# A hybrid attention trunk on one core: part of its bulk loads issued on ScalarE's queue and not on SyncE's

## The chip, the core and the metric

The kernel runs on one core of a Trainium2 chip. A core has a matrix engine (TensorE, "PE" in the rows, with its weight loads as "PEld"), a vector engine (VectorE, "DVE"), an activation engine (ScalarE, "ACT"), a general engine (GpSimd, "POOL") and SyncE ("SP"), which computes nothing and here issues the transfers. Each engine works through its own instructions in the order in which they were laid out, and an instruction that waits for a semaphore holds up those behind it. The transfers themselves are carried by 16 DMA engines. "PEq", "SPq" and "ACTq" in the rows are the instruction queues of the engines. The metric is the time of one execution of the whole program in microseconds (us).

## What is computed

One layer on 1024 rows of 1024 numbers, in float32: a root-mean-square norm, one input projection, two groups of mixers side by side, an output projection with a residual add, a dense SwiGLU feed-forward part, and a last norm.

```python
h = rms_norm(x, attn_norm)
a_conv, q, kc_r, vc_r, ks, vs, kw, vw, g = jnp.split(h @ w_in, splits, axis=-1)
conv_out = conv_mixer(a_conv, conv_w, conv_b, conv_ln_g, conv_ln_b)
kc = compress(kc_r, cmp_k_pe, cmp_k_w1, cmp_k_w2)
vc = compress(vc_r, cmp_v_pe, cmp_v_w1, cmp_v_w2)
nsa_out = nsa_attention(q, kc, vc, ks, vs, kw, vw, sigmoid(g))
x = x + concatenate([conv_out, nsa_out]) @ w_out
h = rms_norm(x, ffn_norm)
gate, up = jnp.split(h @ w_gate_up, 2, axis=-1)
return rms_norm(x + (silu(gate) * up) @ w_down, final_norm)
```

The attention has 12 query heads in 4 groups and three gated branches: over compressed blocks, over the 8 best blocks of 64 keys, and over a window of 512 keys, each with a distance penalty.

## The kernel before

A float32 operand of a matmul is split into a rounded part and a rest (`w_hi` and `w_lo`, `ph` and `pl`), and a product is three matmuls. `load_w` (L214) brings weights: it takes one of two `w_raw` buffers, loads 512 KB into it by a transfer that SP issues (L224), lets ACT round it (L225) and POOL subtract, in four pieces (L229). In the first half of the attention POOL first writes one column of the buffer from a result of the attention (L220), so that loads do not run far ahead of it. `Feed` (L193) asks for loads up to two ahead of the one in use.

The stages in order of time: norm, transposes and the first half of the projections; then the attention (`attention`, L678), woven by `weave` (L175) with other matrix work that fills TensorE. The attention has 64 steps: half of the rows (`part`), group, query tile of 128 rows and branch. A step loads its keys and values when they change (L697 to L706) and its queries (`q`, L713 to L720); scores (L756 to L760), minimum (DVE, L764), exponential (ACT, L767), scaling by gate and sum (POOL, L777); then for each block of 128 keys a transpose into PSUM (L783), a split by ACT and DVE (L233) and two products (L800, L801), which stand two blocks behind the transpose (`LAG = 2`, L816). `cmp_stage` (L597) makes the compressed branch and stores it (L644), to be loaded again as `pct` (L727).

The fill is `fill_all` (L1339): first `fill_b` (L938), the second half of the projections, with 18 loads of `w_in` in 22 transfers, stores of the results by SP (L299, L429), then the output projection of the first half of the rows: `mix_in` (L1034) loads the mixed rows, `x_in` (L1020) the residual rows in 8 transfers of 256 KB, `out_loads` 8 loads of `w_out`, `load_row` (L1083) the norm's row, and then feed-forward work (`ffn`). Nearly all of the transfers of the whole program are issued by SP, whatever their size.

The order in which each engine gets its instructions is worked out when the program is built, by a scheduler that plays the program through with modelled times (`schedule_with_timeline_sim=True`) and, when an engine is free, takes what is ready, first that which stands first in the source. So an edit in one place can shift the order elsewhere.

Of the kernel before, what the change touches and what calls it, by code (L numbers as in the profile page):

```python
# [19 lines left out]
P = 128  # L20
# [68 lines left out]
def tile_hymba(ctx: ExitStack, tc, x, attn_norm, w_in, conv_w, conv_b, conv_ln_g, conv_ln_b,  # L89
# [3 lines left out]
    dve, act, pool, pe, sp = nc.vector, nc.scalar, nc.gpsimd, nc.tensor, nc.sync  # L93
# [116 lines left out]
        return bank(name, turn[1][turn[0] % len(turn[1])])  # L210

    pace = []

    def load_w(parts, a, b, eng=pool):  # L214
        raw = wp.tile([P, WCH], F32, tag="raw", name="w_raw", bufs=2)
        hi = wp.tile([P, WCH], F32R, tag="whi", name="w_hi")
        lo = wp.tile([P, WCH], F32R, tag="wlo", name="w_lo")
        back = PACE_B if phase[0] == 0 else PACE_C
        if len(pace) >= back > 0:
            pool.tensor_copy(raw[:, 0:1], pace[-back][:, 0:1])  # L220
        n = a * b
        v = raw[:, :n].rearrange("p (k c) -> p k c", k=a)
        for c, src in parts:
            sp.dma_start(v[:, :, c:c + src.shape[-1]], src.rearrange("(k p) c -> p k c", p=P))  # L224
        act.copy(hi[:, :n], raw[:, :n])  # L225
        step = n // PIECES if eng is pool else n
        for c in range(0, n, step):
            q = slice(c, c + step)
            eng.tensor_sub(lo[:, q], raw[:, q], hi[:, q].bitcast(F32))  # L229
        return (hi[:, :n].rearrange("p (k c) -> p k c", k=a), lo[:, :n].rearrange("p (k c) -> p k c", k=a))  # L230
# [4 lines left out]
    def norm_rows(dst, src, grow, p, tmp):  # L235
        ss = p.tile([P, 1], F32, tag="ss", name="ss", bufs=4)
        act.activation(tmp, src, AF.Square, accum_out=ss)
        rs = p.tile([P, 1], F32, tag="rs", name="rs", bufs=4)
        dve.tensor_scalar(rs, ss, 1.0 / DM, EPS, op0=ALU.mult, op1=ALU.add)
        pool.tensor_tensor(rs, rs, mhalf, op=ALU.pow)  # L240
        dve.scalar_tensor_tensor(dst, src, rs, grow, op0=ALU.mult, op1=ALU.mult)
        return rs

    def transpose_tile(src, hhi, hlo, col, tag="t"):
        for jj in range(2):
            b = bank("tp", tag)
            for k in range(4):
                pe.transpose(b[:, k * P:(k + 1) * P], src[:, (jj * 4 + k) * P:(jj * 4 + k + 1) * P], ident)
            b3 = b.rearrange("p (k t) -> p k t", k=4)
            done = split(hhi[jj][:, :, col:col + P], hlo[jj][:, :, col:col + P], b3)  # L250
        return done
# [24 lines left out]
    def win_chunk(c0):  # L276
        return load_w([(0, w_in[0, :, c0:c0 + P])], KT, P)


    def value_loads(c0, g0, eng=pool):  # L280
        return [lambda kh=kh: load_w([(0, w_in[0, kh * 512:(kh + 1) * 512, c0:c0 + 256]),
                                      (256, w_in[0, kh * 512:(kh + 1) * 512, C_G + g0:C_G + g0 + 18])], 4, 274, eng)
                for kh in range(2)]
# [23 lines left out]
    def values(feed, g0, dst, hf):  # L307
        ws = [feed.get(), feed.get(1)]
        for t in range(hf * 4, hf * 4 + 4):
            yield from value_tile(ws, g0, dst, t)  # L310
        value_gates(g0, hf)
# [103 lines left out]
    def project_d(feed, dst, row, halves, scaled=False):  # L415
        wh, wl = feed.get()
        for hf in halves:
            o = acc_bank("zo")
            yield from gemm_t(o, wh, wl, hf)
            zh = p1.tile([P, 512], F32R, tag="zh", name="zh", bufs=2)  # L420
            zl = p1.tile([P, 512], F32R, tag="zl", name="zl", bufs=2)
            if scaled:
                sc = qsc[:, row // P:row // P + 1]
                act.mul(zh, o, sc)
                dve.scalar_tensor_tensor(zl, o, sc, zh.bitcast(F32), op0=ALU.mult, op1=ALU.subtract)
            else:
                split(zh, zl, o)
            for i, z in ((0, zh), (1, zl)):
                sp.dma_start(dst[i, row:row + P, hf * 512:(hf + 1) * 512], z.bitcast(F32))  # L429
# [86 lines left out]
    def conv_loads():  # L516
        return [lambda c=c: win_chunk(c) for ct in range(2) for c in (CONV + ct * P, ct * P)]

    def conv_in(feed, hf, wide=False):
        y = py.tile([P, 2, 30 + 512], F32, tag="y", name="y")  # L520
        pool.tensor_copy(y[:, :, 0:30], tail)
        for ct in range(2):
            os = []
            for s in range(2):
                os.append(acc_bank("cv"))
                wh, wl = feed.get()
                yield from gemm_t(os[s], wh, wl, hf)
            sg = p1.tile([P, 512], F32, tag="zh", name="sg", bufs=2)
            act.activation(sg, os[0], AF.Sigmoid)
            dve.tensor_mul(y[:, ct, 30:], os[1], sg)  # L530
        if hf == 0:
            pool.tensor_copy(tail, y[:, :, 512:])
        ys[hf] = y
# [326 lines left out]
    def q_load(m):  # L860
        return lambda: win_chunk(C_Q + m * P)

    def kv_loads():
        return [lambda c=c, m=m: win_chunk(c + m * P) for m in range(2) for c in (C_KW, C_KS)]
# [70 lines left out]
    pc_stack, pc = open_pool("pc", "right")  # L935
    turn[1] = "z"

    def fill_b():  # L938
        f1 = Feed([q_load(0), q_load(1)] + value_loads(C_VS, 0) + [q_load(2)] + value_loads(C_VW, 18)
                  + [q_load(m) for m in (3, 4, 5)] + kv_loads() + conv_loads())  # L940
        for m in (0, 1):
            yield from project_d(f1, q_d, m * P, (1,), True)
        yield from values(f1, 0, vs_d, 1)
        done.add(("q", 0))
        yield from project_d(f1, q_d, 2 * P, (1,), True)
        done.add(("q", 1))
        yield from values(f1, 18, vw_d, 1)
        done.update({("v", 0), ("v", 1)})
        for m in (3, 4):
            yield from project_d(f1, q_d, m * P, (1,), True)  # L950
        done.add(("q", 2))
        yield from project_d(f1, q_d, 5 * P, (1,), True)
        done.add(("q", 3))
        for dst in (kw_d, ks_d):
            yield from project_d(f1, dst, 0, (1,))
        done.add(("kv", 0))
        for dst in (kw_d, ks_d):
            yield from project_d(f1, dst, P, (1,))
        done.add(("kv", 1))
        yield from conv_in(f1, 1)  # L960
        done.add(("conv", "in"))
# [53 lines left out]
    def set_in(si, p):  # L1015
        acts[si] = p
        pairs = [p.tile([P, 2, DM], F32, tag="x1", name="x1", bufs=2) for _ in range(2)]
        x1s[si] = [pairs[j // 2][:, j % 2, :] for j in range(4)]

    def x_in(si, ch):  # L1020
        h = slice(ch * 512, (ch + 1) * 512)
        for t, x1 in zip(SETS[si], x1s[si]):
            sp.dma_start(x1[:, h], x[0, t * P:(t + 1) * P, h])

    def set_norm(si, p):
        pools[si] = p
# [3 lines left out]
    def mixed(si, kq):  # L1030
        return ("conv", si) in done and all(("mix", g, i) in done for g in range((2, GROUPS)[kq]) for i in SETS[si])
# [49 lines left out]
                    dve.tensor_tensor(xs, o, xs, op=ALU.add)  # L1081

    def load_row(row, vec):  # L1083
        sp.dma_start(row, vec.partition_broadcast(P))


    def norm_space(p):
        a, b = [p.tile([P, 2, DM], F32, tag="act", name="rows", bufs=2) for _ in range(2)]
        return a[:, 0, :], (a[:, 1, :], b[:, 0, :], b[:, 1, :])

    def ffn_norm_in(si, tag):
        grow, xns = norm_space(acts[si])
        load_row(grow, ffn_norm[0])
        for t, x1 in enumerate(x1s[si]):
            xn = xns[t % 3]
            norm_rows(xn, x1, grow, pools[si], xn)
            yield 4.0
            transpose_tile(xn, h2[si][0], h2[si][1], t * P, tag)
            yield 0.9
# [239 lines left out]
    def fill_all():  # L1339
        yield from fill_b()  # L1340
        while not mixed(0, 0):
            yield -1.0
        mix = mix_in(0, 0, pm)
        set_in(0, pm)
        x_in(0, 0)
        x_in(0, 1)
        yield LEAD_C
        yield from out_proj(feed, 0, "z", mix, 0)

        while not mixed(0, 1):  # L1350
            yield -1.0
        p1_stack.close()
        last["p3"], p = open_pool("p3", "left")
        mix2 = mix_in(0, 1, p, "h21")
        yield from out_proj(feed, 0, "z", mix, 1)
        yield MIXLAT
        for ch in range(2):
            yield from out_proj(feed, 0, "z", mix2, ch)
        set_norm(0, p)
        yield from ffn_norm_in(0, "z")  # L1360
        for _ in range(NF // 2):
            yield from ffn(feed, (0,), FT)

# [81 lines left out]
```

## Time and profile before

| | |
|---|---|
| median of 3 runs | 1490.61 us (1489.68 to 1493.18) |
| the profiled execution | 1491.48 us |
| its span in the trace | 1489.8 us |
| mean granted clock of TensorE | 0.982 of full speed |
| TensorE busy | 1432.4 us (96%) |
| bytes moved | 196.86 MB, mean 132 GB/s |

The trace covers the span; the rest of the profiled execution's time lies around it. A busy share tells little by itself here, since the stages differ: a row of "windows" shows what each engine did in one stretch, and the granted clock beside it. At a granted clock of 1.00 TensorE runs at 2.4 GHz; a stretch with less has some time at 1.2 GHz in it. The chain of waits names, going back from the last instruction, what released each step. Times of a transfer run from its issue to its landing.

### The profile page before, as it was taken

Reading aid. Unit: us, or ns where it says so; the run is one execution under the profiler, and the core shown is the slowest. Engines: PE = TensorE matmul, PEld = TensorE weight load, DVE = VectorE, ACT = ScalarE, POOL = GpSimd, SP = SyncE. Lnnn points to the kernel's source line nnn. Section 1 sums busy time; section 2 is a strip of 40 time slices with the busy share of each in tenths; the row PEclk is TensorE's granted clock in tenths of the full one; section 3 lists DMA queues with packets and bytes.
Section 4 is the critical chain, followed back from the end, with each engine's and each line's share of the span. In section 5 each row is a group of like instructions: output and inputs, shape, how many; then the busy total and the mean of one; then the engine's idle time right before and its main releaser. Section 6 shows DMA issues by size and latency. Waiting matters only on the chain.

```text
span 1489.8 us, 23548 instructions
## 1 busy us (share of the span) xinstructions
PE 1432.4 (96%) x7991; PEld 1241.7 (83%) x7991; DVE 1014.7 (68%) x2243; ACT 799.1 (54%) x1629; POOL 690.3 (46%) x971
## 2 busy tenths in 40 slices
PE   7999989999999999999999999999999899999997
PEld 7788878877778878888888888878887799999996
DVE  6992465768767677677676776321738888888885
ACT  6233577768766576656566565412425344444443
POOL 4766463766766455665555556645557000000001
PEclk9999999999989999999999999999999899999999
DMA  7336477667578434335344313733244332333321
GB/s 231 87 95 198 132 212 231 168 191 187 168 247 224 124 91 113 96 104 131 89 106 113 97 49 93 249 116 133 71 128 144 108 115 87 114 86 107 108 70 71
DMA packets 238676, 196.86 MB, mean 132 GB/s; under 512 B 15976, under 2 KB 208332, under 8 KB 238556
## 3 DMA queue, kind: packets, MB, share of 16 engines
q1 hardware_dynamic: 238556, 195.36, 45.0%
q8 instruction: 63, 1.03, 0.3%
q14 instruction: 57, 0.47, 0.1%
HBM read 161.56 MB, written 33.75 MB: 131 GB/s over the span
## 4 chain that ended last, share of the span: by engine, by line
PE 73%; DVE 10%; DMA 6%; ACT 3%; POOL 3%; issue 3%; SPq 0%; ACTq 0%; POOLq 0%; DVEq 0%
PE gu L1121 15%; PE dn L1140 14%; PE yy L1245 8%; PE pt L783 4%; PE zo L145 4%; PE zz L1245 4%; PE wo L1055 3%; DVE cacc L553 3%; PE s L756 3%; PE o L800 2%; PE o L801 2%; PE wo L1076 2%; PE vo L145 2%; PE aa L1245 2%; POOL w_lo L229 2%
## 5 line engine op out<-in xcount | busy, mean ns | idle before, releaser
L229 POOL TENSOR_TENSOR w_lo<-w_raw,w_hi 128x256 fp32r<-128x256 f32 (+1 forms) x504 | 402.6, 830 | 187.1 <-ACT w_hi L225 173.2
L1121 PE MATMUL gu<-h,w_hi 128*128 128x512 f32 x768 | 251.8, 398 | 0.5 <-DVE x L1145 0.5
L1140 PE MATMUL dn<-w_hi,aw 128*128 128x512 f32 x688 | 241.6, 398 | 8.5 <-DVE aw L233 7.1
L225 ACT CAST w_hi<-w_raw 128x1024 fp32r<-128x1024 f32 (+1 forms) x147 | 152.6, 1049 | 130.7 <-PE gu L1121 48.8
L777 POOL TENSOR_SCALAR pr<-pr,l,gates 128x640 f32<-128x640 f32 (+5 forms) x192 | 150.9, 798 | 98.2 <-DVE l L772 87.9
L767 ACT ACTIVATE pr<-pr,m 128x640 f32<-128x640 f32 (+5 forms) x192 | 141.5, 737 | 84.4 <-DVE m L764 77.7
L1121 PEld LDWEIGHTS gu<-h,w_hi 128*128 128x128 f32 x768 | 143.2, 188 | 29.6 <-DVE x L1145 1.0
L233 DVE TENSOR_TENSOR pl<-pt,ph 128x384 fp32r<-128x384 f32 x264 | 139.1, 549 | 36.4 <-ACT ph L233 35.0
L1140 PEld LDWEIGHTS dn<-w_hi,aw 128*128 128x128 f32 x688 | 129.7, 189 | 34.9 <-DVE aw L233 7.5
L1318 POOL TENSOR_TENSOR rs<-rs,mhalf 128x1 f32<-128x1 f32 x4 | 2.6, 644 | 327.5 <-DVE rs L1317 327.3
L233 ACT CAST ph<-pt 128x384 fp32r<-128x384 f32 x264 | 117.3, 477 | 67.5 <-PE pt L783 55.4
L1121 PE MATMUL gu<-h,w_lo 128*128 128x512 f32 x384 | 152.2, 396 | 0.0
L1145 DVE TENSOR_TENSOR x<-dn,x 128x512 f32<-128x512 f32 x176 | 118.5, 683 | 48.2 <-PE dn L1140 47.2
L783 PE MATMUL pt<-ident,pr 128*128 128x128 f32 x792 | 137.5, 273 | 0.5 <-POOL pr L777 0.2
L1140 PE MATMUL dn<-w_lo,aw 128*128 128x512 f32 x344 | 136.1, 396 | 0.0
L764 DVE CUSTOM_DVE_ANT_0 pr<-s,base 128x384 f32<-128x384 f32 (+3 forms) x192 | 101.3, 533 | 27.4 <-PE s L760 14.9
L1196 ACT CAST w_s<-sum 128x512 fp32r<-128x512 f32 x80 | 49.4, 621 | 123.1 <-PE yy L1245 100.2
L783 PEld LDWEIGHTS pt<-ident,pr 128*128 128x128 f32 x792 | 101.7, 140 | 16.3 <-POOL pr L777 1.8
L145 PE MATMUL zo<-h,w_hi 128*128 128x512 f32 x320 | 109.1, 408 | 3.8 <-ACT af L475 2.3
L756 PE MATMUL s<-kt,q 128*128 128x384 f32 (+3 forms) x288 | 100.5, 352 | 5.8 <-DMA q<-q_d 3.6
L800 PE MATMUL o<-ph,vt 128*128 128x384 f32 x264 | 99.1, 375 | 0.3 <-ACT ph L233 0.3
L1245 PEld LDWEIGHTS yy<-term,w_s 128*128 128x128 f32 x720 | 94.7, 191 | 5.3
(260 smaller groups left out, 3159.8 us busy)
## 6 DMA issues: line engine op xcount, KB each, us to landing
w_raw<-in_w_gate_up_dram SPq DMA_DIRECT2D x48, 512.0 KB, 3.8
w_raw<-in_w_down_dram SPq DMA_DIRECT2D x43, 512.0 KB, 3.6
w_raw<-in_w_in_dram SPq DMA_DIRECT2D x40, 512.0 KB, 5.4
u_raw<-in_w_gate_up_dram SPq DMA_DIRECT2D x20, 512.0 KB, 5.1
g_raw<-in_w_gate_up_dram SPq DMA_DIRECT2D x19, 512.0 KB, 3.9
q<-q_d SPq DMA_DIRECT2D x80, 96.0 KB, 3.4
qc<-q_d SPq DMA_DIRECT2D x32, 192.0 KB, 4.2
pc_d<-pct SPq DMA_DIRECT2D x16, 384.0 KB, 3.2
```

Source lines behind the costliest of these rows:

```text
L145: lastpe[0] = pe.matmul(*args, **kw)
L225: act.copy(hi[:, :n], raw[:, :n])
L229: eng.tensor_sub(lo[:, q], raw[:, q], hi[:, q].bitcast(F32))
L233: return act.copy(hi, src), dve.tensor_sub(lo, src, hi.bitcast(F32))
L756: pe.matmul(sv, q2[:, 0, r, :], kk_[:, 0, kk], start=True, stop=False)
L767: act.activation(pr[:, :n], pr[:, :n], AF.Exp, bias=m, scale=-1.0, accum_out=l3[:, r:r + 1])
L777: pool.tensor_scalar(x_, x_, l3[:, r2:r2 + 1], gates[:, i, c:c + 1], op0=ALU.mult, op1=ALU.mult)
L783: pe.transpose(pt[:, r * P:(r + 1) * P], prs[st][1 + r][:, kk * P:(kk + 1) * P], ident)
L800: pe.matmul(o[:, :384], v, ph, start=False, stop=False)
L1121: pe.matmul(o, w[:, k, :], h2[si][h][k // 4][:, k % 4, :], start=n == 0, stop=n == 3 * KT - 1)
L1140: pe.matmul(o, aws[si][:, a, k, t * P:(t + 1) * P], b[:, 0, ch * 512:(ch + 1) * 512], start=n == 0, stop=n == 5)
L1245: pe.matmul(o, w[:, k, :], h[:, k, :], start=fresh and n == 0, stop=n == 11, skip_group_check=not fresh)
```

## The change

A one-element list `bulk` holds the engine that issues bulk loads. It is SP at first, is set to ACT when the attention begins (just before `fill_b` is defined), and back to SP after the norm of the first half's feed-forward part has been laid out. `load_w`, `x_in` and `load_row` issue on it. All other transfers (queries, keys, values, `pct`, `mix`, all stores) stay on SP. No transfer is added or taken away.

```diff
     pace = []
+    bulk = [sp]
...
         for c, src in parts:
-            sp.dma_start(v[:, :, c:c + src.shape[-1]], src.rearrange("(k p) c -> p k c", p=P))
+            bulk[0].dma_start(v[:, :, c:c + src.shape[-1]], src.rearrange("(k p) c -> p k c", p=P))
         act.copy(hi[:, :n], raw[:, :n])
...
     turn[1] = "z"
 
+    bulk[0] = act
+
     def fill_b():
...
         for t, x1 in zip(SETS[si], x1s[si]):
-            sp.dma_start(x1[:, h], x[0, t * P:(t + 1) * P, h])
+            bulk[0].dma_start(x1[:, h], x[0, t * P:(t + 1) * P, h])
...
     def load_row(row, vec):
-        sp.dma_start(row, vec.partition_broadcast(P))
+        bulk[0].dma_start(row, vec.partition_broadcast(P))
...
         set_norm(0, p)
         yield from ffn_norm_in(0, "z")
+        bulk[0] = sp
         for _ in range(NF // 2):
             yield from ffn(feed, (0,), FT)
```

## Rows read from the trace of the kernel before

**Rows 1.** The page, part 1: busy time, share of the span and instructions of each engine.

```profile
PE 1432.4 (96%) x7991; PEld 1241.7 (83%) x7991; DVE 1014.7 (68%) x2243; ACT 799.1 (54%) x1629; POOL 690.3 (46%) x971
```

**Rows 2.** Windows by stage: the stretch and its length, then busy time and instructions of PE, PEld, DVE, ACT and POOL, the granted clock, the DMA share and GB/s.

```profile
225.00:260.00 35.00, 33.12 (x215) 29.71 (x213) 18.93 (x69) 25.26 (x76) 13.64 (x23) 1.00 0.78 236
...
340.00:380.00 40.00, 36.31 (x187) 29.00 (x186) 33.81 (x126) 31.89 (x100) 28.73 (x48) 0.91 0.71 188
...
460.00:500.00 40.00, 37.22 (x208) 32.30 (x207) 26.91 (x77) 22.18 (x49) 18.20 (x25) 0.96 0.79 225
...
600.00:700.00 100.00, 100.00 (x540) 86.53 (x540) 70.46 (x177) 65.74 (x117) 62.04 (x85) 1.00 0.39 106
```

**Rows 3.** What TensorE waited for between 220 and 540 us: total us, times, longest.

```profile
PE s L756 <- DMA q<-q_d: 3.6, 2, 2.5
PE wo L1055 <- DMA mix<-mix_d: 2.8, 2, 2.0
PE s L760 <- DMA kt<-ks_d: 1.8, 1, 1.8
...
PE zo L145 <- DMA pct<-pc_d: 0.6, 1, 0.6
```

**Rows 4.** The same view of three short stretches, 260 to 268, 350 to 362 and 472 to 486 us, one row of each.

```profile
PE s L756 <- DMA q<-q_d: 1.2, 1, 1.2
...
PE s L756 <- DMA q<-q_d: 2.5, 1, 2.5
...
PE wo L1055 <- DMA mix<-mix_d: 2.0, 1, 2.0
```

**Rows 5.** Windows of 5 us, columns as in group 2.

```profile
260.00:265.00 5.00, 4.07 (x18) 2.48 (x18) 4.39 (x16) 3.72 (x10) 2.88 (x5) 1.00 1.01 278
265.00:270.00 5.00, 3.83 (x26) 3.36 (x26) 2.43 (x9) 5.00 (x14) 5.00 (x8) 1.00 0.49 142
...
355.00:360.00 5.00, 2.42 (x10) 1.98 (x11) 1.83 (x10) 4.64 (x16) 4.39 (x8) 0.78 0.82 260
360.00:365.00 5.00, 5.00 (x19) 4.16 (x18) 3.48 (x16) 3.20 (x9) 3.54 (x7) 0.54 0.19 57
...
480.00:485.00 5.00, 5.00 (x16) 3.96 (x16) 0.14 (x1) 0.07 (x1) 0.68 (x1) 0.66 1.18 319
```

**Rows 6.** The chain of waits between 210 and 545 us: start, us, what. For a transfer the us run from its issue to its landing.

```profile
261.04 5.68 DMA q<-q_d
...
352.53 5.96 DMA q<-q_d
...
402.53 3.76 DMA w_raw<-in_w_in_dram
...
415.95 3.79 DMA w_raw<-in_w_in_dram
...
474.32 5.45 DMA mix<-mix_d
...
491.70 3.92 DMA mix<-mix_d
```

**Rows 7.** The timeline of SP's queue: start, us of the issuing instruction, line, transfer, how many in a row.

```profile
212.42 2.46 SPq L224 DMA_DIRECT2D w_raw<-in_w_in_dram  x4
...
258.61 1.01 SPq L224 DMA_DIRECT2D w_raw<-in_w_in_dram  x2
...
350.43 0.45 SPq L224 DMA_DIRECT2D w_raw<-in_w_in_dram  x1
...
473.93 0.34 SPq L1084 DMA_DIRECT2D rows<-in_ffn_norm_dram  x1
```

**Rows 8.** Line L714 (the second query transfer of a step) between 185 and 545 us: issue to landing; and the page's part 3, the queue that carries the kernel's own transfers: packets, MB, share.

```profile
DMA to landing us min/median/max: 2.5/3.5/5.7
...
q1 hardware_dynamic: 238556, 195.36, 45.0%
```

**Rows 9.** Lines L224 and L1023 between 185 and 545 us (issuing instructions: shortest, median and longest in ns, first and last start), and the residual loads on SP's timeline.

```profile
L224 SPq DMA_DIRECT2D w_raw<-in_w_in_dram x23: 367/415/552, 190.6 to 415.9; - x23
...
L1023 SPq DMA_DIRECT2D x<-in_x_dram x8: 328/430/1178, 429.4 to 440.3; - x8
...
429.36 0.45 SPq L1023 DMA_DIRECT2D x<-in_x_dram  x1
...
432.94 2.20 SPq L1023 DMA_DIRECT2D x<-in_x_dram  x4
...
436.59 4.01 SPq L1023 DMA_DIRECT2D x<-in_x_dram  x3
```

**Rows 10.** ScalarE and the room behind it: windows of 200 to 485 and of 205 to 210 us; what TensorE waited for between 198 and 225 us; the transposes of line L783 between 225 and 545 us (three for each block of keys); the roundings of loaded weights between 200 and 485 us (us busy, mean ns, then idle time before them by what ended it).

```profile
200.00:485.00 285.00, 264.68 (x1459) 225.37 (x1458) 198.66 (x653) 202.28 (x557) 177.87 (x272) 0.95 0.71 201
...
205.00:210.00 5.00, 1.91 (x7) 1.51 (x8) 4.77 (x17) 4.91 (x9) 4.07 (x6) 0.76 0.66 179
...
PE zo L145 <- ACT af L475: 2.3, 1, 2.3
...
L783 PE MATMUL pt<-ident,pr x318: 270/272/421, 247.7 to 539.6; 128*128 128x128 f32 x159
...
L225 ACT CAST w_hi<-w_raw 128x1024 fp32r<-128x1024 f32 (+1 forms) x25 | 26.2, 1053 | 15.0 <-DMA w_raw<-in_w_in_dram 9.9 <-PE wo L1055 2.0 <-DMA w_raw<-in_w_out_dram 1.6
```

**Rows 11.** What SP's queue waited for between 200 and 500 us, the one row of a moved load's buffer: total us, times, longest.

```profile
SPq L224 <- POOL w_raw L220: 12.3, 3, 7.4
```

## The prediction

> **What bounds the kernel now.** I read the page's first part: TensorE is busy for 96% of the span [rows 1]. So there are only some 57 us without a matmul, and time is to be won where such gaps lie, or where the clock falls after one. Next the windows by stage: from 600 to 700 us TensorE has no gap and a full clock, while the stretch that the change touches, 200 to 485 us, has gaps and a granted clock of 0.91 to 1.00 [rows 2]; over its 285 us TensorE is busy 264.7 us at 0.95 [rows 10]. The work after it waits for TensorE alone, so a gap that goes here shortens the whole, and one that comes here lengthens it. Third, what ends TensorE's gaps: transfers end 3.6 + 2.8 + 1.8 + 0.6 = 8.8 us of them, queries and mixed rows first [rows 3]. The short stretches say where: 1.2 us at 261, 2.5 us at 356 and 2.0 us at 478 us [rows 4]. Fourth, windows of 5 us show what a gap costs beyond itself: the granted clock reads 0.78 and 0.54 around the gap at 356, 0.66 after that at 478, and 1.00 through that at 261 [rows 5]. A mean of 0.54 is a stretch most of which ran at 1.2 GHz after TensorE had stood still.
>
> **What is moved.** 40 transfers go from SP's queue to ACT's: the 22 of `fill_b`, 8 of `w_out`, 8 of `x_in`, the norm's row, and the first gate load, which `Feed` asks for ahead of its use. Nothing is removed: the bytes, their buffers and the waits before them stay, and only the queue in which each stands is another.
>
> **What it can give: small transfers no longer behind bulk.** In the chain the three costly waits have a bulk transfer issued just ahead of them [rows 6, 7]:
> - Queries issued at 261.04 landed after 5.68 us; two loads had been issued at 258.61. The median of that line is 3.5 us [rows 8]; the 2.2 us between cover the gap of 1.2 us. Gain 1.2 us (0 to 1.2).
> - Queries at 352.53 took 5.96 us behind a load of 350.43. At 3.5 us they are 2.5 us earlier, which is the gap, 2.5 us. The clock goes with it: 0.22 x 2.42 + 0.46 x 5.00 = 2.8 us of full-speed work lost in the two windows [rows 5]. Gain 5.3 us (0 to 5.3).
> - Mixed rows at 474.32 took 5.45 us behind the 512 KB of the norm's row at 473.93; those at 491.70, with no bulk just ahead, took 3.92 [rows 6]. That is 1.5 us of the 2.0, and 0.34 x 5.00 = 1.7 us of clock. Gain 3.2 us (0 to 3.7).
>
> The other gaps for transfers (keys at 242 us, the second mixed rows) have no bulk ahead and stay. Sum 9.7 us, 0 to 10.2.
>
> All of the kernel's transfers run on one hardware queue [rows 8], so no row shows two side by side; whether a small transfer passes a bulk one on another queue is the open point, and the bounds above are nothing and all. I take nearly all, since the fast cases of the same lines lie so close by. The Trainium skill (DMA: Bandwidth & Descriptors, section "Queues, rings and completion order") says that each DMA engine goes round between the queues that have work, packet by packet; that would let the small transfer through and is not shown by any run here.
>
> **What it costs: ACT's own order.** An issue took SP 0.415 us in the median [rows 9], and so 40 of them 16.6 us, on an engine that is busy 202.3 of 285 us [rows 10]. What hides them is the room behind ACT. There are 318 transposes, three a block, in 292 us: a block each 2.75 us, and products stand two blocks behind, 5.5 us. The transpose, the two halves of the split and the product's start take about 1.5 us of it, so ACT may be late by some 4 us before TensorE stands (an estimate from [rows 10]). So single issues cost nothing; without that cover all 16.6 us would show. Who would wait: behind a held ACT stand exponentials and splits, then POOL's scaling and the transposes. Four places where it can show:
> - The start. From 205 to 210 us ACT is busy 4.91 of 5 us and TensorE waits 2.3 us for it [rows 10]. Into that stretch fall the four issues at 212.42, 2.46 us on SP [rows 7], and one more of 0.42: 0 to 2.9 us. I take 1.5, the middle, since TensorE has fill work soon after.
> - The residual rows: eight issues that become free together, at the median 8 x 0.43 = 3.4 us, as measured on SP 0.45 + 2.20 + 4.01 = 6.7 us [rows 9]. Beyond 4 us: 0 to 2.7, and a clock fall of 2.8 at worst. I take 1.3.
> - The waits for a free buffer, now on ACT. SP stood 12.3 us in three waits for POOL's column, the longest 7.4 [rows 11]. The planner puts an issue into ACT's order about where it becomes free, so I take 0; the upper end is 7.4 - 4 = 3.4 and a clock fall, 6.2.
> - The loads themselves. Sharing the engines, they land later: ACT already waits 9.9 us for them [rows 10], and two landings of 3.8 us stand in the chain [rows 6]. 0 to 2.0, taken 1.0, as two short delays.
>
> SP's other queue neighbours (stores of `fill_b`, `pct`, keys) lose only what stood in front of them; POOL gets no instruction. The new order of the planner may also shift work that has nothing to do with this; no row bounds that but the spread of the cases below.
>
> **Sum.** -9.7 + 1.5 + 1.3 + 0 + 1.0 = -5.9 us. The profiled execution took 1491.48 us for a span of 1489.8, and the median of the runs is 1490.61, so the profile stands for the median within 0.9 us: 1490.6 - 5.9 = about 1485 us. Its own range runs from 1479 (all the gains with the late loads' 1.0 as the only cost: -10.2 + 1.0 = -9.2, and some luck of order) to 1488.
>
> **The rivals.**
> Only the issue time is saved: the bulk transfer still goes first on the same 16 engines. Then a query is earlier only by the issues ahead of it, 1.01, 0.45 and 0.34 us [rows 7], the clock falls stay, and the sum is -1.8 + 1.5 + 1.3 = +1.0: 1491.6 us, no difference. For it: the engines' share reads 1.01 in the window of the first case and 1.18 in the third's [rows 5], so bytes may be what the small transfer waits for. Against it: the queue at 491.70 served the same kind of transfer in 3.92 us [rows 6]. The Trainium skill (DMA: Bandwidth & Descriptors, section "Issuing engines are not separate DMA queues") states this rival: all issuing engines share the same DMA engines, and several only save issue time. By that rule the change gives nothing; the trace, with one queue, can't settle it.
>
> ACT stands in its own queue: from the point at which ACT is held for more than 4 us at a bulk issue, exponentials and splits come late, TensorE stops and its clock falls. At the upper ends: start 2.9, residual rows 2.7 + 2.8, a buffer's wait 6.2, late loads 2.0, together 16.6 against 9.7 of gain: +6.9, so 1497.5 us. For it: the 7.4 us and 6.7 us that SP has stood at just these issues [rows 9, 11]. Against it: ACT idles 83 of 285 us [rows 10].
>
> The planner's new order outweighs both, without any of these mechanisms: somewhere from 1476 to 1498.
>
> **How the numbers follow.** Forecast 0.50, issue time only 0.20, ACT held 0.18, new order 0.12. About 0.2%, 3 us, is what a measurement of this kernel can tell from no change: faster is below 1487.6, slower above 1493.6. The forecast gives 0.48 faster and 0.02 same; the second 0.16 same, 0.02 to each side; the third 0.03 same and 0.15 slower; the last 0.04, 0.04, 0.04. Sum: faster 0.54, same 0.25, slower 0.21. The range for 8 in 10 takes in the rival at 1497.5 and, below, the forecast's best with some of the free order: 1476 to 1498.
>
> **What would show it.** Right: a second hardware queue with the 40 transfers; queries at about 350 us landing in 3.5 us, TensorE's waits for transfers of 3.6 + 2.8 us mostly gone, and no windows of 0.54 and 0.66 at these places. Wrong in the first way: the same landings of 5 to 6 us with another queue. Wrong in the second: ACT's idle time ended by POOL's column or by nothing before an issue, with TensorE's waits for `ph` or `pr` grown, above all where the residual rows are loaded. The prediction is wrong as a whole if the stretch from 200 to 540 us keeps its length, or if the gain lies after it.

## The result and the profile after

The changed kernel takes 1511.23 us in the median of 5 runs (1508.12 to 1513.3), beside 1490.61 us for the kernel before (5 runs, 1486.58 to 1493.18): a ratio of 1.0129 with a 95% interval of 1.011 to 1.0148. It is 20.6 us slower, where 5.6 us less was forecast, and lies outside the range. The profiled execution took 1508.85 us for a span of 1507.1.

The page of the changed kernel: the first line of its part 1 and two lines of its part 3 (queue, packets, MB, share of the engines' span).

```profile
PE 1434.9 (95%) x7991; PEld 1236.5 (82%) x7991; DVE 1015.8 (67%) x2243; ACT 793.2 (53%) x1625; POOL 688.8 (46%) x971
...
q1 hardware_dynamic: 215260, 178.43, 41.0%
q10 hardware_dynamic: 23296, 16.93, 4.3%
```

A second queue is there, with the bytes of the 40 transfers. TensorE does the same work (1434.9 us busy, 1432.4 before [rows 1]) in a longer span: 1507.1 - 1434.9 = 72.2 us without a matmul, where it was 57.4. To see where, windows of the changed kernel, first one that answers to one of before, then two longer ones; in the second fence the longer ones of the kernel before. Columns as in group 2.

```profile
340.00:380.00 40.00, 37.55 (x214) 31.22 (x213) 34.20 (x120) 30.97 (x99) 29.97 (x49) 1.00 0.74 199
...
380.00:540.00 160.00, 143.32 (x750) 120.96 (x749) 109.79 (x329) 100.66 (x240) 90.22 (x126) 0.96 0.62 168
880.00:1100.00 220.00, 211.24 (x955) 168.58 (x954) 88.01 (x151) 75.03 (x120) 116.69 (x159) 1.00 0.40 119
```

```profile
380.00:540.00 160.00, 151.25 (x805) 127.99 (x804) 115.84 (x342) 106.31 (x250) 94.62 (x134) 0.96 0.62 179
880.00:1100.00 220.00, 219.08 (x1016) 179.53 (x1015) 98.35 (x174) 80.23 (x128) 125.88 (x169) 1.00 0.39 122
```

Three things are to be seen. From 340 to 380 us the clock is 1.00 where it was 0.91 [rows 2]: the gap at 356 us is gone, as forecast. From 380 to 540 us TensorE is busy 7.9 us less than before. And from 880 to 1100 us, where no bulk load is on ACT's queue any more, it is busy 7.8 us less, in a stretch that had lost 0.9 us of 220.

To compare kernels whose orders differ I count the work done from 180 us on: each matmul of a stretch, from the view of groups with their shapes kept apart, at its columns by 2.4 GHz (512 columns are 0.213 us), and the float32 transposes at twice that, since three of 128 columns take 0.33 us in the chain. Beside the kernel before at the same moment the changed kernel is 6.5 us ahead at 380 us, 7.7 behind at 480, 4.3 behind at 740 and 15.1 behind at 1110. So there is an early loss (up to 740 us, the attention's first half with its fill) and a late one (740 to 1110 us, the attention's end and the feed-forward part after it), of 4.3 and 10.8 us.

What TensorE waited for in the changed kernel, first between 380 and 545 us, then between 880 and 1110; total us, times, longest.

```profile
PE o L796 <- DVE ou L806: 5.8, 4, 2.1
PE o L801 <- ACT ph L234: 3.7, 3, 1.8
PE wo L1058 <- DMA mix<-mix_d: 2.1, 1, 2.1
...
PE s L761 <- DMA kt<-kw_d: 0.8, 1, 0.8
PE s L757 <- DMA kt<-kw_d: 0.7, 1, 0.7
```

```profile
PE dn L1143 <- DVE x L1148: 3.5, 4, 1.7
PE tp L249 <- DVE rows L242: 2.1, 3, 0.9
PE wo L1079 <- DMA mix<-mix_d: 1.6, 3, 1.1
PE tp L249 <- DVE rs L240: 0.6, 1, 0.6
```

Early, the attention's products wait for ACT and for what follows it (`ph`, `ou`); late, `dn` and the transposes `tp` of the second half's norm wait for VectorE. The two rows of the kernel before for the late stretch are `tp` 0.4 us and one wait for ACT of 0.4 us. Two of the early waits, 2.1 us for `ou` at 439 us and 1.8 us for `ph` at 447 us, come just after stands of ACT; where the other 5.6 us of those two rows come from is open. ACT's timeline in the changed kernel (start, us, what; in brackets the idle time before it and its releaser):

```profile
433.84 3.30 ACTq L1026 DMA_DIRECT2D x<-in_x_dram  x2
437.18 0.48 ACT L234 CAST ph<-pt 128x384 fp32r<-128x384 f32 x1 [3.71 <-DMA x<-in_x_dram]
...
444.62 0.39 ACTq L225 DMA_DIRECT2D w_raw<-in_w_out_dram  x1
445.05 0.51 ACT L808 CAST oh<-ou 64x384 fp32r<-64x384 f32 x1 [2.14 <-DMA x<-in_x_dram]
```

ACT stood 3.7 and 2.1 us, and the releaser is the landing of a residual transfer, which neither instruction reads. The built program says why. All transfers of both queues count on the same eight counters (the landings in the trace are on eight, too), and an issue first waits until the earlier transfer on its counter has landed. The eight residual loads had four counters between them, so the last four waited for the first four. It holds the other way too. What SP's queue waited for in the changed kernel, 425 to 460 us:

```profile
SPq L704 <- DMA w_raw<-in_w_out_dram: 4.4, 1, 4.4
...
SPq L702 <- DMA x<-in_x_dram: 3.1, 1, 3.1
```

Key loads on SP (L702, L704) stood until bulk loads of the other queue had landed.

### The profile page after: what moved, and what is told of

Read it like the earlier page. It is cut to its first block, busy times and chain, and to the rows that moved or that the text cites. A ratio compares the mean times of both kernels' runs of the same rounds, so it can differ in the third digit from the quotient of the medians.

```text
span 1507.1 us, 23542 instructions
## 1 busy us (share of the span) xinstructions
PE 1434.9 (95%) x7991; PEld 1236.5 (82%) x7991; DVE 1015.8 (67%) x2243; ACT 793.2 (53%) x1625; POOL 688.8 (46%) x971
## 4 chain that ended last, share of the span: by engine, by line
PE 68%; DVE 11%; DMA 8%; ACT 5%; issue 3%; POOL 3%; SPq 0%; ACTq 0%; DVEq 0%; POOLq 0%
PE gu L1124 14%; PE dn L1143 13%; PE yy L1248 8%; PE zo L145 5%; PE pt L784 4%; PE zz L1248 4%; DVE cacc L554 3%; PE wo L1079 3%; PE wo L1058 2%; PE vo L145 2%; PE o L802 2%; PE o L801 2%; PE s L757 2%; PE aa L1248 2%; DMA w_raw<-in_w_in_dram 2%
## 5 line engine op out<-in xcount | busy, mean ns | idle before, releaser
L226 ACT CAST w_hi<-w_raw 128x1024 fp32r<-128x1024 f32 (+1 forms) x147 | 152.8, 1050 | 162.1 <-PE gu L1124 50.0
L1148 DVE TENSOR_TENSOR x<-dn,x 128x512 f32<-128x512 f32 x176 | 118.0, 683 | 33.2 <-PE dn L1143 32.7
```

## The experiments

All ratios are to runs of the kernel before on the same chip, with 95% intervals. "Early" and "late" are the losses from 180 to 740 us and from 740 to 1110 us in work done, as above, from each kernel's one profiled execution, which can lie some us off the median (E16: 1493.6 against 1497.6; E11: 1490.6 against 1495.2).

| kernel | bulk on ACT's queue | order of the engines | median us | ratio | early | late |
|---|---|---|---|---|---|---|
| changed | all | its own | 1511.2 | 1.0129 [1.011, 1.0148] | 4.3 | 10.8 |
| E1 | all | before's | 1497.7 | 1.0042 [1.0023, 1.0062] | 5.5 | 1.1 |
| E2 | none | changed's | 1528.7 | 1.0267 [1.0227, 1.0307] | 20.9 | 11.5 |
| E3 | weights | free | 1509.6 | 1.0135 [1.0085, 1.0186] | 2.0 | 12.4 |
| E4 | rows | free | 1494.9 | 1.0038 [1.0012, 1.0063] | 2.5 | 1.0 |
| E5 | all | changed's, late part before's | 1508.1 | 1.0108 [1.0085, 1.0132] | 14.1 | 1.1 |
| E6 | none | before's, late part changed's | 1514.1 | 1.0158 [1.0138, 1.0177] | 7.3 | 14.9 |
| E7 | projections | free | 1498.2 | 1.0046 [1.0029, 1.0062] | 3.0 | 6.9 |
| E8 | projections | as E7, late part before's | 1491.0 | 0.9995 [0.9979, 1.0011] | 0.4 | 1.2 |
| E9 | all, rows in two | free, late part before's | 1495.7 | 1.0029 [1.0009, 1.0048] | 5.3 | 1.7 |
| E10 | weights | as E3, late part before's | 1497.8 | 1.0037 [1.0019, 1.0055] | 4.8 | -0.3 |
| E11 | weights | before's | 1495.2 | 1.0031 [1.001, 1.0052] | 0.6 | 0.1 |
| E12 | projections, rows in two | free, late part before's | 1492.7 | 1.0007 [0.9985, 1.0028] | 1.7 | 3.5 |
| E13 | weights | E5's | 1503.7 | 1.0085 [1.0059, 1.011] | 9.8 | 0.7 |
| E14 | all, rows in two | E5's | 1498.7 | 1.0043 [1.0024, 1.0061] | 10.5 | 0.8 |
| E15 | weights | changed's | 1511.0 | 1.0118 [1.0083, 1.0153] | 6.5 | 11.8 |
| E16 | none | E5's, SP's too | 1497.6 | 1.0048 [1.0027, 1.0068] | 2.5 | -0.4 |
| E17 | none | changed's, SP's too | 1509.0 | 1.0124 [1.0091, 1.0158] | 3.7 | 11.2 |
| E18 | E5 measured again | | 1500.6 | 1.0044 [1.0029, 1.006] | 8.5 | 1.1 |

An order is held by edges without a wait: each engine's instructions, by their names in the source's order, are chained as another kernel has them. In short:

```diff
     pd_stack.close()
+    for names in order.values():
+        for a, b in zip(names, names[1:]):
+            tc.add_manual_dep(traced[b], a, NoSync, reason="order")
```

**The queue with the old order, the old queue with the new order (E1, E2).** E1 is the change plus the chains of the kernel before on TensorE, VectorE, ScalarE and GpSimd; E2 is the kernel before plus the changed kernel's chains.

> The 40 transfers on ACT's queue as in the changed kernel, but the order of instructions on TensorE, DVE, ACT and POOL held to that of the kernel before, instruction by instruction; only the places of the 40 issues in ACT's order are free. Theory A (ACT stands in its own queue: at the burst of residual loads, 3.7 us, and at roundings that wait for their own load, 24.0 us in 14 waits against 11.8 in 8): the loss stays, 1500 to 1512 us. Theory B (the planner's new order makes the loss, as after 880 us where no bulk load is on ACT any more): no loss, 1482 to 1493 us. If both hold in halves, as the work done by 540 us and by 1100 us suggests (7 and 11 us behind): about 1498 us.

> The counterpart: all transfers on SP's queue as in the kernel before, but the order of instructions on TensorE, DVE, ACT and POOL held to that of the changed kernel. Theory A: about the time of before, 1488 to 1496 us, since ACT issues nothing. Theory B: the loss stays, 1503 to 1515 us. In halves: about 1501 us, with the stretch after 880 us as slow as in the changed kernel and the stretch before 540 us as fast as before.

E1 came out at the time for "both in halves". It has next to no late loss (1.1 us) and 6.3 us in all (0.0042 of 1490.6): the price of the queue where the engines keep the order of before, with SP's own order free (the transfers that stay on SP differ from before's order by swaps of neighbours alone). E2 has the late loss, with no transfer on ACT: the late loss goes with the order. E2's early loss is its own, since SP's order had been left free and brought a load of `w_out` late; none of its three times came out. What ACT waited for in E2 between 430 and 500 us:

```profile
ACT w_hi L225 <- DMA w_raw<-in_w_out_dram: 24.8, 1, 24.8
```

So E2 prices no early order; E16 and E17 mend that.

**One kind of load alone (E3, E4).**

```diff
-            bulk[0].dma_start(x1[:, h], x[0, t * P:(t + 1) * P, h])
+            sp.dma_start(x1[:, h], x[0, t * P:(t + 1) * P, h])
...
-        bulk[0].dma_start(row, vec.partition_broadcast(P))
+        sp.dma_start(row, vec.partition_broadcast(P))
```

That is E3; E4 has these two on `bulk[0]` and `load_w` on SP.

> Only the weight loads on ACT's queue (31 transfers); residual rows and the norm's row stay on SP. The planner's order is free. Theory A with the burst of residual loads as its place: 5 to 8 us faster than the changed kernel, 1503 to 1506 us; with late loads as its place: 1508 to 1512 us. Theory B: any time between 1485 and 1515 us, without relation to what is moved.

> Only the residual rows and the norm's row on ACT's queue (9 transfers); all weights stay on SP. The planner's order is free. Theory A with the burst as its place: 1494 to 1500 us; with late loads as its place: 1488 to 1493 us. Theory B: any time between 1485 and 1515 us.

The two are no halves of the change: E3 alone is as slow as the whole. Its planned order has the late part with `tp` between `dn` matmuls, as the changed kernel's has; E4 kept the late order of before and has next to no late loss (1.0 us).

**Only the late order (E5, E6).** The chains hold only what stands in the source behind the first `gu` matmul; E5 is the change with those of before, E6 the kernel before with those of the change.

> The 40 transfers on ACT's queue as in the changed kernel. All that stands in the source behind the first matmul of the first half's feed-forward part is held to the order of the kernel before on TensorE, VectorE, ScalarE and GpSimd; what stands ahead of it keeps the changed kernel's order. Theory (order): the loss of some 11 us between 880 and 1100 us is the planner's other order there, so it goes: 1511 - 11 = about 1500 us, and TensorE's matmuls between 880 and 1100 us are 955 again, 211 us busy or the like with no waits for VectorE's adds. What is left of the loss, about 9 us, is that of 440 to 480 us. Rival (delay): the late loss is a consequence of the earlier holds, whatever the order: 1508 to 1513 us.

> The kernel before, all bulk loads on SP's queue; only the order of what stands in the source behind the first matmul of the first half's feed-forward part is that of the changed kernel, on the four computing engines. Theory (order): about 1491 + 11 = 1502 us without a single transfer on ACT, with the loss between 880 and 1100 us and waits of TensorE for VectorE's adds there. Rival (delay): within 0.2% of the kernel before, 1488 to 1494 us.

The late loss went from 10.8 to 1.1 us in E5 and came with 14.9 in E6, on SP's queue alone. In this the theory held. But E5's time fell by only 3.1 us, as its early loss was 14.1, though up to some 490 us it runs the very program of the changed kernel; and E6 was slower than either theory said, since the late order, set beside the early order of before, also lost 7.8 us from 540 to 640 us.

**Fewer loads on ACT (E7, E8).** E3, with `load_w` set back to SP where `fill_b` ends; E8 adds the late chains of before.

```diff
-        yield from fill_b()
+        yield from fill_b(); bulk[0] = sp
```

> Only the 22 transfers of the second half's projections on ACT; the loads of w_out, the residual rows and the norm's row on SP; the planner free. Theory: ACT is not held at 430 to 446 us, so the loss there is smaller than the 11.6 us of the changed kernel, and the lead of 5.5 us at 380 us stays in part; if the planner gives the late order of the changed kernel, the 11 us of 880 to 1100 us are lost all the same: 1491 - 5 + 11 = about 1497 us. Rival: the weights' loads are what holds ACT, and the loss at 440 to 480 us stays as in the changed kernel: 1507 to 1511 us.

> As the kernel with only the 22 transfers of the second half's projections on ACT, and what stands in the source behind the first feed-forward matmul held to the order of the kernel before. Theory (order): 11 us less than that kernel where it had the changed kernel's late order, so about 1486 us, faster than both kernels by some 4 us. Rival (delay): the same time as that kernel. If the loss at 440 to 480 us comes with any early order that leads, the lead of 5 us is lost again and it is 1491 us.

E7 came out near its theory's 1497 us. At the same queues the late order costs 1498.2 - 1491.0 = 7.1 us in the medians. With it put right, E8 takes the time of before: of its three cases the last, 1491 us, came out. Its order up to the feed-forward part is the planner's own, so E8 shows the 22 transfers together with that order, and the two together bring neither a loss nor a gain that can be measured; by its interval a gain would be 3.1 us at most, where the prediction put 6.5 on the first two of its three cases, whose bulk is loads of the projections. E8 is the fastest of the variants and no faster than the kernel before.

**Merged rows, and rows on SP (E9 to E12).** In E9 and E12 one transfer of 1 MB brings two tiles of residual rows, two issues and not eight; in short:

```diff
-        for t, x1 in zip(SETS[si], x1s[si]):
-            bulk[0].dma_start(x1[:, h], x[0, t * P:(t + 1) * P, h])
+        for j, two in enumerate(pairs0[:2 * (ch == 0)]):
+            bulk[0].dma_start(two, x[0, j * 2 * P:(j + 1) * 2 * P, :].rearrange("(j p) c -> p j c", p=P))
```

E9 is the change with this and the late chains, E10 is E3 with the late chains, E11 is E3 with all chains of before, E12 has the projections' loads, the merged rows and the norm's row on ACT, with the late chains.

> All bulk loads on ACT as in the changed kernel, the feed-forward part held to the order of the kernel before, and the eight residual transfers of 256 KB laid together into two of 1 MB: same bytes, two issues, and in the built program neither of them waits for the landing of an earlier residual transfer on its counter. Theory (ACT is held by landings): ACT no longer stands 3 to 4 us at a residual issue, and most of the early loss of 13 us goes: 1493 to 1499 us against 1508. Rival (bytes): the loss comes from transfers that share the engines, and it stays: 1505 to 1510 us.

> The weights (second half's projections and w_out) on ACT, residual rows and norm's row on SP, the feed-forward part held to the order of the kernel before. Theory (ACT is held at the residual rows): 1490 to 1497 us against 1508 with the rows on ACT, since ACT issues no residual row. Rival (bytes, or the loads of w_out on ACT): 1505 to 1510 us.

> The weights on ACT, residual rows and norm's row on SP, and all four computing engines held wholly to the order of the kernel before, as in the kernel that had all 40 transfers on ACT in that order and took 1497.7 us. Theory (residual rows): its loss of 6 us goes, 1490 to 1493 us. Rival (weights): the loss stays, 1496 to 1499 us.

> The 22 transfers of the second half's projections and the residual rows as two transfers of 1 MB on ACT, the loads of w_out on SP, the feed-forward part held to the order of the kernel before. Theory (ACT is held by landings, and only there does the move cost): 1486 to 1491 us, no worse than the 1491.0 us with the rows on SP. Rival (bytes): 1495 us or more, since the rows again share the engines with the mixed rows.

E9 falls into its theory's range, E10 0.8 us above it, E11 and E12 between their two. All are faster than E5 by 10 to 15 us, which spoke for ACT's stand at the rows. It did not hold up: E18 below moves E5 itself to 1500.6, and then E9's and E10's intervals overlap with it. E11 (1.001 to 1.0052) can't be told from E1 (1.0023 to 1.0062) either, so what the rows cost on ACT in before's order stays open.

**The same order, the rows moved or merged (E13 to E15).** E13 is E3 with all of E5's chains, E14 is E9 with them, E15 is E3 with all of the changed kernel's.

> Residual rows and norm's row on SP, the weights on ACT, and the four computing engines held instruction by instruction to the order of the kernel that had everything on ACT with the late order of before and took 1508.1 us. Between the two only the queue of nine transfers differs (and where SP's own order puts them). Theory (ACT is held at the rows): 1493 to 1500 us, and TensorE's waits for ph between 430 and 460 us go. Rival (the early order itself is the loss): 1505 to 1510 us.

> The same order of the four computing engines again, all 34 bulk transfers on ACT, the residual rows as two transfers of 1 MB and not eight of 256 KB. Theory (ACT is held at the rows, chiefly by the landings of the first four): 1494 to 1501 us, and one hold of some 4 us left, at the next load of w_out. Rival (early order): 1505 to 1510 us.

> The changed kernel's own order on the four computing engines from end to end, with the residual rows and the norm's row on SP. Theory: the hold of ACT goes and the late order stays, 1511 less 5 to 9 us: 1501 to 1507 us, with the loss of some 11 us between 880 and 1100 us as before. Rival: if the late order costs only because of the earlier hold, 1491 to 1497 us; if the rows on ACT cost nothing, 1509 to 1513 us.

E14 falls into its theory's range, E15 into that of "the rows on ACT cost nothing", E13 between its two ranges. None decides. With the rows on SP and SP's order free, they came late and VectorE stood for them (what it waited for in E13, 430 to 480 us):

```profile
DVE x L1059 <- DMA x<-in_x_dram: 10.6, 1, 10.6
```

E14 still has ACT stand, at another place. Its timeline there:

```profile
457.98 0.37 ACTq L224 DMA_DIRECT2D w_raw<-in_w_out_dram  x1
458.40 0.51 ACT L807 CAST oh<-ou 64x384 fp32r<-64x384 f32 x1 [9.04 <-DMA kt<-kw_d]
```

Here ACT stood 9.0 us at the issue of a weight load, until a key load of SP's queue had landed. In the built program this issue waits for that key load's counter, and for nothing else that the keys have to do with.

**The queue and nothing else (E16, E17).** All bulk loads on SP, the four engines chained to E5's order (E16) or the changed kernel's (E17), and SP's own transfers chained too, each bulk load in the place that it has in that kernel's program.

> All 40 transfers on SP. The computing engines are held instruction by instruction to the order of the kernel that had the 40 on ACT and the late order of before (1508.1 us), and SP issues all transfers in the order in which that kernel's program has them, so each bulk load stands where it stood, only on the other queue. Theory (ACT is held at its issues): ACT's holds of 3 to 4 us at 436 to 452 us go, SP stands there instead, 1493 to 1500 us. Rival (the early order itself, or small transfers late behind SP's stands): 1505 to 1512 us.

> The same with the changed kernel's own order from end to end: all 40 transfers on SP at the places where the changed kernel's program has them, the four computing engines in the changed kernel's order. It differs from the changed kernel by the queue alone. Theory (ACT held early, late order on its own): 1500 to 1506 us, the loss of some 11 us between 880 and 1100 us stays. Rival (order is all of it): 1509 to 1514 us.

E16 falls into its theory's range, E17 to the lower end of its rival's, "order is all of it". E17 is the changed kernel without its second queue, and takes 1509.0 us to its 1511.2; by the ratios 0.05% lie between them, inside both intervals. So nearly all of the loss, 18.5 of 19.2 us (0.0124 and 0.0129 of 1490.6), is there without one transfer on ACT. The interval of E17 is 13.6 to 23.6 us, and the two kernels ran on different occasions, so this comparison alone can't price the queue to better than some us. E17 and E16 ran on the same chip and differ by the late order alone: 1509.0 - 1497.6 = 11.4 us. What TensorE waited for between 880 and 1110 us, in E17 and then in E16 (its only row there):

```profile
PE dn L1140 <- DVE x L1145: 3.3, 4, 1.4
PE tp L248 <- DVE rows L241: 2.5, 3, 1.3
PE wo L1076 <- DMA mix<-mix_d: 2.4, 2, 1.3
```

```profile
PE tp L248 <- DVE rows L241: 0.4, 1, 0.4
```

Without ACT's stands TensorE waits for transfers instead. The same view of E17 from 380 to 545 us:

```profile
PE wo L1055 <- DMA mix<-mix_d: 4.8, 2, 3.1
PE s L756 <- DMA kt<-kw_d: 2.9, 1, 2.9
PE o L795 <- DVE ou L805: 2.5, 3, 1.0
PE s L760 <- DMA kt<-kw_d: 2.0, 1, 2.0
PE o L800 <- ACT ph L233: 1.9, 2, 1.3
```

On SP's queue it is 9.7 us for mixed rows and keys and 4.4 us for `ou` and `ph`; on ACT's queue, in the changed kernel's rows above, 3.6 and 9.5. One wait took the other's place, 14.1 us in sum and 13.1.

**E5 once more (E18).** The same kernel on another chip, 12 runs.

> The kernel with the 40 transfers on ACT and the late order of before once more, on whatever chip this call has. It and the changed kernel run the same instructions in the same order up to some 490 us, and yet the profile of the one had lost 15.2 us by 480 us and that of the other 7.7. If the queue costs some 10 us with this order: 1505 to 1510 us again. If what an ACT queue costs is scattered from one execution and chip to the next: 1498 to 1503 us, nearer to the 1497.6 us that the same order took with SP's queue.

1500.6 us, ratio 1.0044 [1.0029, 1.006], where E5 had 1.0108 [1.0085, 1.0132]: two intervals of the same kernel that don't touch; it is the case of scatter. Beside E16 (1.0048) the queue then costs nothing in this order either; beside the first measurement it costs 0.6%. So the queue's own price is 0.4% with the order of before (E1), nothing to 0.6% with E5's order and 0.05% with the changed kernel's; in no order is it a gain beyond the noise. What separates E5's two measurements stays open.

## Why the prediction was wrong

**The gain, "small transfers no longer behind bulk", 9.7 us: this step failed.** E1 tests it alone: the computing engines keep the order of before, SP's other transfers nearly so, and the bulk is on the other queue. Its rows, first what TensorE waited for between 220 and 540 us, then the landings of line L714, then two windows:

```profile
PE o L795 <- DVE ou L805: 5.0, 1, 5.0
PE s L756 <- DMA q<-q_d: 3.6, 2, 3.0
PE wo L1055 <- DMA mix<-mix_d: 3.5, 3, 2.1
...
DMA to landing us min/median/max: 2.6/3.4/6.7
...
340.00:380.00 40.00, 35.70 (x182) 28.33 (x181) 33.35 (x122) 31.06 (x98) 28.12 (x46) 0.91 0.66 186
360.00:365.00 5.00, 5.00 (x18) 4.24 (x18) 3.80 (x12) 2.65 (x8) 4.46 (x9) 0.50 0.37 106
```

Before it was 3.6 and 2.8 us for queries and mixed rows [rows 3], landings of 2.5/3.5/5.7 [rows 8], and a clock of 0.91 and 0.54 in these windows [rows 2, 5]. The waits and the fall of the clock that the 9.7 us were added up from are still there. In the changed kernel, too, TensorE waits 2.3 us for queries and 2.1 us for mixed rows between 220 and 540 us. The queries were issued between two loads of ACT's queue (255.97 and 256.80 us), and their row in the chain of waits is:

```profile
256.78 6.92 DMA q<-q_d
```

The changed kernel and E17 differ by the queue alone, so their landings can be laid side by side. DMA issues between 200 and 545 us (count, KB each, median us from issue to landing), first the changed kernel, then E17:

```profile
q<-q_d SPq DMA_DIRECT2D x47, 96.0 KB, 3.8
...
mix<-mix_d SPq DMA_DIRECT2D x8, 256.0 KB, 5.3
...
mix<-mix_d SPq DMA_DIRECT2D x4, 512.0 KB, 5.9
```

```profile
q<-q_d SPq DMA_DIRECT2D x47, 96.0 KB, 4.1
...
mix<-mix_d SPq DMA_DIRECT2D x8, 256.0 KB, 4.9
...
mix<-mix_d SPq DMA_DIRECT2D x4, 512.0 KB, 4.6
```

With the bulk on another queue the queries land 0.3 us sooner, and the mixed rows 0.4 and 1.3 us later. The other kinds differ both ways, from 0.7 us sooner (256 KB of keys, 8.2 to 7.5) to 1.9 us later (residual rows, 4.8 to 6.7). The prediction had named this as its open point and had taken "nearly all" since fast cases of the same lines lay close by; those cases showed that a query can land in 3.5 us, not that the queue was what kept the others. What came in its place is twofold: the engines carry both queues' bytes as they did one's (from 380 to 540 us a share of 0.62 and 168 GB/s, in E17 0.62 and 172), and by the shared counters SP still stands for bulk loads (4.4 and 3.1 us above). The first rival, "only the issue time is saved", had the mechanism right for the gain. The Trainium skill (DMA: Bandwidth & Descriptors, section "Issuing engines are not separate DMA queues") has that result, and the landings agree with it; the turns packet by packet of its section "Queues, rings and completion order" are neither shown nor refuted by medians, but the gain that the prediction drew from them is not there.

**The gap at 356 us and the clock.** In the changed kernel both went as the forecast said, and for another reason, so that sign came true by luck. E1, with the order of before, still has the gap (3.0 us) and the clock of 0.91; E17, with the new order, has no such gap and a clock of 1.00 from 340 to 380 us, on SP's queue:

```profile
340.00:380.00 40.00, 36.17 (x206) 30.50 (x205) 33.68 (x122) 31.83 (x102) 29.14 (x48) 1.00 0.68 188
```

The new order moved the work around that query. At 380 us E16 and E17 are 4.9 and 3.8 us ahead of before without a transfer on ACT, the changed kernel 6.5, E5 and E18, with its program up to there, 1.6 and 4.6. The lead goes with the order, and scatters by some 5 us from one execution to another.

**ACT's own costs: the start 1.5, residual rows 1.3, buffers 0, late loads 1.0.** At the start nothing showed: at 220 us the changed kernel was 1 us ahead in work done. No wait of ACT between 200 and 545 us was ended by POOL's column, so 0 for the buffers was right. ACT waited longer for the loads, 19.8 us between 200 and 545 us where it had been 9.9 [rows 10]; but it is 21.0 in E17 on SP's queue, so that too came with the order. The residual rows were sized by their issue time, 3.4 to 6.7 us on SP, less 4 us of room; the stand was 3.7 + 2.1 us and came from landings, not from issues. With the order of before it was 5.7 us at one place (E1, released by a residual row's landing at 434.7 us), and the wait of 5.0 us for `ou` in the rows above follows it at 437 us: there the rival "ACT stands in its own queue" is seen at work, and that its 1497.5 us meets E1's 1497.7 is luck, since it was added up from four upper ends. With the changed kernel's order the net price is small, since with SP's queue keys and mixed rows are waited for instead (E17).

**"The planner's new order outweighs both": the right case, with the wrong price and chance.** It was put at 1476 to 1498 us with 0.12, from "the spread of the cases", that is, from costs of other mechanisms, and in the forecast's own sum it stood at nothing. This is the second step that failed, and the larger: the order alone, on SP's queue, takes 1509.0 us (E17), 18.5 of the 19.2 us. It has two parts. Held to the late order of before, 7.2 us are left (E16, 0.0048 of 1490.6), the price of the new early order. The profiled execution of E16, 4 us under its median, loses 8.9 us in work done from 440 to 480 us, regains 6.0 by 540 and loses 3.9 more by 640; from 380 to 545 us TensorE waits for mixed rows and keys in it, where before waited 2.8 us for mixed rows [rows 3] and for no keys of this stretch:

```profile
PE wo L1055 <- DMA mix<-mix_d: 5.1, 2, 2.9
PE s L756 <- DMA kt<-kw_d: 2.6, 1, 2.6
```

The late order costs the other 11.4. Of TensorE's waits of the late stretch in the changed kernel, 8.5 us, 4.7 fall before 1000 us: 2.8 for adds on VectorE in runs of `dn` matmuls, 1.6 for mixed rows and 0.3 for `aw`. The other 3.8 fall between 1050 and 1075 us. TensorE's timeline in the changed kernel, where the second half's norm is transposed:

```profile
1054.03 1.09 PE L249 MATMUL tp<-ident,rows 128*128 128x128 f32 x8 [0.88 <-DVE rows L242]
1055.70 0.66 PE L249 MATMUL tp<-ident,rows 128*128 128x128 f32 x4 [0.58 <-DVE rs L240]
1056.36 0.50 PE L1143 MATMUL dn<-w_hi,aw 128*128 128x512 f32 x1
...
1060.10 1.06 PE L249 MATMUL tp<-ident,rows 128*128 128x128 f32 x8 [0.54 <-DVE rows L242]
```

And in the kernel before:

```profile
1058.73 0.60 PE L248 MATMUL tp<-ident,rows 128*128 128x128 f32 x4
1059.09 0.72 PE L1121 MATMUL gu<-h,w_hi 128*128 128x512 f32 x2
...
1061.03 1.04 PE L248 MATMUL tp<-ident,rows 128*128 128x128 f32 x8
```

Before, most of the transposes (20 of 32) stand between `gu` matmuls, 24 to a bank, and one wait of 0.4 us is all that the norm's rows cost. In the changed kernel all of them stand between `dn` matmuls, six to a bank, each bank followed by an add on VectorE (`x`, L1148); the norm's rows and the adds take turns on VectorE, and TensorE waits for both. That order appears in every kernel with a late loss over 6 us (in E7, which lost 6.9, for 24 of the 32 transposes) and in no other. So the late order as a whole is shown as the cause (E16 and E17); that the place of the transposes and the runs of `dn` make its loss is read from the waits. That the plan changed is shown; what made the planner choose it stays open.

The row that should have widened the range was at hand: TensorE busy 100.00 of 100 us from 600 to 700 [rows 2]. A stretch with no gap has nothing to win from another order and everything to lose, so the "free order" case ought not to have been drawn evenly around the time before.

## What to carry to other kernels

Where a planner lays out the order, an edit's first effect is another order: hold the old order to see what the edit does, and the old queue in the new order to see what the order does, before a mechanism is believed. A kernel tuned to a gapless order has mostly downside in any shuffle, in stretches that the edit doesn't touch: of the variants here none was faster than before beyond its interval. A second issuing queue was no second path here: look at whether landings shorten, and at which counters its issues must wait for, above all when the issuer is an engine that computes.

## What the runs showed that was not expected

A compute engine that issues transfers can stand for a landing of the other queue: 9.0 us at a weight load until a key load had landed (E14), and SP 4.4 us for a weight load of ACT's. Twenty-two issues on ACT, on the other hand, cost nothing on balance (E8). And the interval of one measurement was narrower than the difference between chips or occasions: the same kernel gave 1.0108 [1.0085, 1.0132] and 1.0044 [1.0029, 1.006].
